# x rows of the gate and up stage in four buffers on one side, its factors emitted in turn with them, and the residual loads on GpSimd's queue

## The chip, the cores and the metric

One core of a Trainium2 chip runs the whole program. The metric is device time in microseconds (us), the median of the runs shown. Every time below is from one profiled execution of the kernel before, counted from the start of its span, if nothing else is said.

## What is computed

One layer of a hybrid decoder over 2048 prompt tokens (with 16 meta tokens ahead of them) and 32 sample tokens, all in float32. The change touches what comes after the two mixing branches are merged into `mix`:

```python
mix = (sigmoid(ga) * br_a + sigmoid(gb) * br_b) @ w_out
x = x + rms_norm(mix, norm_mix_post)
f = rms_norm(x, norm_ffn_pre)
f = (silu(f @ w_ffn_gate) * (f @ w_ffn_up)) @ w_ffn_down
x = x + rms_norm(f, norm_ffn_post)
```

D_MODEL is 1024 and D_FF is 2816. A float32 product is made of three matmuls: each operand is split into a high part (rounded to fp32r) and a low part (the rest), and high by high, high by low and low by high are summed (`mm3`, L156 to L163; in two stages written out).

## The kernel before

The stages run one after the other: projection, convolution and the two branches, merge, **way out**, **gate and up**, **down**. TensorE (PE) is busy in nearly all of them.

**Way out** (L1320 on) takes the merged rows `mg_d`, multiplies them by w_out, and goes by groups of rows: first the 32 sample rows, then eight pairs of 128 rows. For each tile `way_rows` loads `mr` (L1356, on SP's queue), splits it into `hh` (L1358, ACT) and `hl` (L1360, DVE), loads the residual rows `xr` (L1363, SP's queue) and does 48 matmuls `psr` (L1370 to L1373). `way_tail` then does a pair: a squared sum `sq` (L1394, ACT), the gain (L1399, DVE), a reciprocal root by ten or so short DVE instructions (L100 to L107), the residual sum (L1404, DVE, into `xr`), the write of y (L1405, POOL's queue), a second norm and its scaling `wa` (L1411, DVE), eight transposes of a tile on PE (L282, `pst`), their copies out `fo` (L286, ACT) and four writes of `f_d` (L287, POOL's queue). The tail of a pair runs while PE multiplies the next pair. Each engine and each queue takes its instructions in the order in which the program was built, which the program's framework makes from the emitted code and from when buffers come free.

**Gate and up** (L1505 on) computes both products with a Strassen-Winograd scheme of seven block products. Its operands are prepared by two generators. `b_parts` (L1427) loads quarters of the normed rows from `f_d` (L1434, tile `fr`, 128 x 4 x 348), splits each (`xh` L1440 on ACT, `xl` L1441 on DVE), and makes the sums that the scheme needs (L1450, L1453, L1458, L1462, DVE); the last of these needs a second load of one quarter. `a_parts` (L1467) loads a column block of both weights (L1482, `araw`) and makes the factors `ah` (L1475, ACT) and `al` (L1476, DVE or POOL), with the sums `S` and `R` (L1488 to L1491, DVE) between. The factors live in a ring of 56 KB a partition, `ar`, which is handed out from its top down; a tile `pad` taken first sets where the first factors come to lie. `gate_up` empties `b_parts` and then `a_parts` before the first step. 33 steps of some 26 us follow (three column pairs by eleven blocks of weights), each with 168 matmuls `psf`; they write `h_d` (L1547).

**Down** (L1595 on) loads rows of h (`hr`, L1621, from `h_d`, 768 KB each), splits them (`hh` L1623 on ACT, `hl` L1628 on DVE) and multiplies by split weights `wu` (`wload`: `wr` loaded at L144, high part at L146 on ACT, low part half on POOL at L148, half on DVE at L149); the matmuls are `psr`, L1637, L1638 and L1640.

The memory of a stage is taken from pools on the left and on the right side of SBUF (`run`, L1719 to L1750). A tile of a later stage may lie on memory of an earlier one, and then its first writer waits for the last reader there. In the kernel before the four buffers of `fr` are two on the right and two, `fr2`, on the left; the left two lie on `wa` tiles of the way out.

Of the kernel before, what the change touches and what calls it, by code (L numbers as in the profile page):

```python
# [7 lines left out]
F32 = mybir.dt.float32  # L8
# [7 lines left out]
P = 128  # L16
D = 1024
NM = 16
SEQ = 2048
# [24 lines left out]
PAIRS = ((0, 348), (696, 348), (1392, 344))  # L44
# [5 lines left out]
def ap_of(t, off, dims):  # L50
    return bass.AP(tensor=t.tensor, offset=t.offset + off, ap=[list(d) for d in dims])
# [19 lines left out]
class Trunk:  # L71
# [1280 lines left out]
    def way_rows(self, r, c):  # L1352
        nc, v = self.nc, self.nc.vector
        wide = r == SMP
        raw = self.wr.tile([P, 1024], F32, tag="wr", name="mr").rearrange("p (k m) -> p k m", k=8)[:, :, :r]
        nc.sync.dma_start(raw, ap_of(self.mg_d, c, [[XW, P], [P * XW, 8], [1, r]]))  # L1356
        hi = self.hh.tile([P, 8, P], F32R, tag="hh", name="hh")
        nc.scalar.activation(hi[:, :, :r], raw, AF.Copy, scale=0.25)  # L1358
        lo = hi[:, :, r:2 * r] if wide else self.hh.tile([P, 8, P], F32R, tag="hl", name="hl")
        v.scalar_tensor_tensor(lo[:, :, :r], raw, 0.25, hi[:, :, :r].bitcast(F32), op0=OP.mult, op1=OP.subtract)  # L1360
        x = self.tm.tile([P, D], F32, tag="tm", name="xr")
        src = self.io["x_prompt"] if c < SEQ else self.io["x_sample"]
        nc.sync.dma_start(x[:r], ap_of(src, c * D if c < SEQ else 0, [[D, r], [1, D]]))  # L1363
        rr = 2 * r if wide else r
        ps = self.pw.tile([P, 2, BLK], F32, tag="pw", name="psr")[:rr]
        for k, (wh, wl) in enumerate(self.wo):
            for half in range(2):
                cs = slice(BLK * half, BLK * half + BLK)
                o = ps[:, half]
                nc.tensor.matmul(o, hi[:, k, :rr], wh[:, cs], start=k == 0, stop=False)  # L1370
                nc.tensor.matmul(o, hi[:, k, :rr], wl[:, cs], start=False, stop=wide and k == 7)
                if not wide:
                    nc.tensor.matmul(o, lo[:, k, :r], wh[:, cs], start=False, stop=k == 7)  # L1373
        ps = ps.rearrange("p a b -> p (a b)")
        if wide:

            t = self.ac.tile([P, D], F32, tag="ac", name="lows")
            nc.scalar.activation(t[:rr], ps, AF.Copy)
            u = self.ac.tile([P, D], F32, tag="ac", name="lowt")
            nc.sync.dma_start(u[:r], t[r:rr])  # L1380
            nc.gpsimd.tensor_add(t[:r], t[:r], u[:r])
            ps = t
        return ps[:r], x, r, c
# [121 lines left out]
    def gate_up(self):  # L1505

        n = FF // 256
        B = None
        for B in self.b_parts(*PAIRS[0]):
            pass  # L1510
        A = [{}, {}]
        for _ in self.a_parts(0, A):
            pass
        order = [(pi, s) for pi in range(3) for s in (range(n) if pi != 1 else range(n - 1, -1, -1))]
        for (pi, s), (pj, sn) in zip(order, order[1:] + [(3, -1)]):
            An, ga = A, None
            if pj < 3 and sn != s:
                An = [{}, {}]
                ga = self.a_parts(sn, An)
            nxt = self.b_parts(*PAIRS[pj]) if pi < pj < 3 else None  # L1520
            Bn = self.gate_up_step(s, *PAIRS[pi], A, B, nxt, ga)
            A, B = An, Bn or B

    def gate_up_step(self, s, c0, w, A, B, nxt, ga):
        nc, v, gp = self.nc, self.nc.vector, self.nc.gpsimd
# [144 lines left out]
    def run(self):  # L1670
        nc, io = self.nc, self.io
        flat = lambda n: io[n].rearrange("o k n -> (o k) n")
        self.w_in, self.w_ga, self.w_gb = flat("w_in"), flat("w_s5_glu_a"), flat("w_s5_glu_b")
        self.w_go, self.w_o = flat("w_gdn_out"), flat("w_out")
        self.w_fg, self.w_fu, self.w_fd = flat("w_ffn_gate"), flat("w_ffn_up"), flat("w_ffn_down")
        G = 32
        for nm, shape in (("m_d", (17 * MS,)), ("t_d", (3 * P * 1024,)), ("on_d", (512, XW)),
                          ("zg_d", (20 * P, XW)), ("tt_d", (G, P, P)), ("wv_d", (G, P, 4, P)),
                          ("cs_d", (G, 64, 2, NL)), ("y_d", (G * 16, 8, YW)),
                          ("u_d", (G * 16, 8, UW)), ("qkv_d", (1536, QW)), ("gct_d", (17, H, P)),  # L1680
                          ("mg_d", (D, XW)), ("f_d", (D, XW)), ("h_d", (FF, XW))):
            setattr(self, nm, self.scratch(nm, shape))
        self.const = self.pool("const", 1)
        kw = dict(reuse_waits="tile")
        self.wp, self.pm, self.wo = Ring(), Ring(), []
        self.pt = self.pool("pt", 2, space=PSUM)
        with ExitStack() as lo:
            self.wr = self.pool("wr", 2, lo)
            self.wp.add(self.pool("wp", 3, lo), 3)
            with ExitStack() as pmx, ExitStack() as pgx:  # L1690
                self.pg = self.pool("pg", 16, pgx, side="right")
                self.pm.add(self.pool("pm", 3, pmx, space=PSUM), 3)
                with ExitStack() as ph:
                    self.tm = self.pool("tm", 4, ph)
                    self.cv = self.pool("cv", 11, ph)
                    self.gd = self.pool("gd", 1, ph)
                    self.small = self.pool("small", 2, ph)
                    self.p1c = self.pool("p1c", 1, ph)
                    self.gp = self.pool("gp", 3, ph, space=PSUM)
                    self.constants()  # L1700
                    self.p1()
                self.wp.add(self.pool("wp2", 5, lo, **kw), 5)
                with ExitStack() as ph:
                    self.wp.add(self.pool("wp4", 4, ph, **kw), 4)
                    self.cv = self.pool("cv2", 7, ph, side="right", **kw)
                    self.pm.add(self.pool("pm2", 3, ph, space=PSUM, **kw), 3)
                    self.merge()
            with ExitStack() as ph:
                self.hh = self.pool("hh", 2, ph, **kw)
                self.ac = self.pool("ac", 2, ph, **kw)  # L1710
                self.tm = self.pool("tm2", 4, ph, **kw)
                self.sq = self.pool("sq", 1, ph, **kw)
                self.fo = self.pool("fo", 2, ph, **kw)
                self.rows = self.pool("rows", 1, ph, **kw)
                self.small = self.pool("small2", 2, ph, **kw)
                self.pw = self.pool("pw", 3, ph, space=PSUM, **kw)
                self.way_out()
        self.pm = self.pool("pm3", 6, space=PSUM, **kw)
        with ExitStack() as ph:  # L1719
            self.gr = self.pool("gr", 2, ph, side="right", **kw)  # L1720
            self.xp = self.pool("xp", 1, ph, side="right", **kw)
            self.fr = Ring()
            self.fr.add(self.pool("fr", 2, ph, side="right", **kw), 2)
            ar = self.pool("ar", 1, ph, side="right", **kw)
            self.ar = ar.ring(56 * 1024, name="ar")
            self.ar.tile([P, 6144], F32, name="pad")
            self.gt = self.pool("gt", 1, ph, **kw)
            self.xq = self.pool("xq", 1, ph, **kw)
            self.xr = self.pool("xr", 1, ph, **kw)
            self.gs = self.pool("gs", 1, ph, **kw)  # L1730
            self.fr.add(self.pool("fr2", 2, ph, **kw), 2)
            self.gate_up()
        with ExitStack() as ph:
            self.wp = Ring()
            self.ac = self.pool("ac3", 9, ph, **kw)
            self.rows = self.pool("rows3", 1, ph, **kw)
            self.lw = self.pool("lw", 1, ph, **kw)
            self.cv = self.pool("cv3", 2, ph, **kw)
            self.small = self.pool("small3", 2, ph, **kw)
            self.wr = self.pool("wr3", 2, ph, side="right", **kw)  # L1740
            self.wp.add(self.pool("wp3", 10, ph, side="right", **kw), 10)
            self.wp.add(self.pool("wp5", 2, ph, **kw), 2)
            self.hh = self.pool("hh", 2, ph, **kw)
            self.hr = self.pool("hr", 2, ph, **kw)
            self.down()
# [202 lines left out]
```

## Time and profile before

| what | value |
|---|---|
| median of 3 runs | 3285.52 us (3281.97 to 3293.22) |
| the profiled execution, its own time | 3288.82 us |
| its span | 3287.0 us |
| PE busy | 3105.4 us, 94% of the span |
| DVE busy | 2015.5 us, 61% |
| ACT busy | 1120.6 us, 34% |
| POOL busy | 910.1 us, 28% |
| mean granted TensorE clock | 0.981 of full speed |
| gate and up stage | about 1833 to 2753 us |

A busy share is a mean over stages. PE is full in the steady part of every stage; the places where it is not are the joints between stages and a few single waits. So a change of this kind is read at the joints: which wait of PE ends last there, and what that instruction had been waiting for.

### The profile page before, as it was taken

How to read it: one execution, taken by the hardware profiler on the slowest of the kernel's cores; microseconds unless marked ns; L12 is line 12 of the kernel's file. 1: busy time of each engine (PE TensorE's matmuls, PEld its weight loads, DVE VectorE, ACT ScalarE, POOL GpSimd, SP SyncE). 2: the span in 40 equal slices, each digit the busy share in tenths (PEclk: the TensorE clock that was granted, in tenths of full speed). 3: DMA queues.
4: the chain of work that ended last, by engine and by line, in shares of the span. 5: the costliest groups of instructions: out<-in, count | busy, mean ns of one | idle time of the engine just before them, and what ended most of it. 6: DMA issues, size and time to landing. Idle time of an engine off the chain costs nothing. (4 is left out here: it accounts for less than half of the span.)

```text
span 3287.0 us, 47621 instructions
## 1 busy us (share of the span) xinstructions
PE 3105.4 (94%) x17461; PEld 2709.1 (82%) x17461; DVE 2015.5 (61%) x4648; ACT 1120.6 (34%) x1944; POOL 910.1 (28%) x903
## 2 busy tenths in 40 slices
PE   6998999999999999999999699999999999999998
PEld 5887778877777777988777699999999998887776
DVE  6888854657897546553444766676676664246235
ACT  4633222433232224221233444444444444223211
POOL 1123441123332212201111344434434444122110
PEclk9999999999999999999999799999999999999999
DMA  5336456545465435653553433333333334235224
GB/s 118 123 101 178 123 156 182 123 122 149 140 190 168 126 110 156 189 158 119 176 180 127 154 104 104 103 121 104 103 103 107 103 103 134 92 102 141 82 59 69
DMA packets 469018, 419.30 MB, mean 128 GB/s; under 512 B 120794, under 2 KB 393370, under 8 KB 468784
## 3 DMA queue, kind: packets, MB, share of 16 engines
q1 hardware_dynamic: 458576, 382.18, 39.9%
q0 software_dynamic: 10208, 34.09, 3.7%
q8 instruction: 137, 2.24, 0.3%
q14 instruction: 97, 0.79, 0.1%
HBM read 288.27 MB, written 127.65 MB: 127 GB/s over the span
## 5 line engine op out<-in xcount | busy, mean ns | idle before, releaser
L161 PE MATMUL psf<-xh,ah 128*128 128x348 f32 (+1 forms) x1848 | 598.8, 324 | 31.9 <-ACT sn L1534 20.2
L163 PE MATMUL psf<-xh,al 128*128 128x348 f32 (+1 forms) x1848 | 593.2, 321 | 6.8 <-DVE al L1476 6.8
L162 PE MATMUL psf<-xl,ah 128*128 128x348 f32 (+1 forms) x1848 | 593.0, 321 | 0.0
L161 PEld LDWEIGHTS psf<-xh,ah 128*128 128x128 f32 x1848 | 348.1, 188 | 41.5 <-ACT sn L1534 29.0
L163 PEld LDWEIGHTS psf<-xh,al 128*128 128x128 f32 x1848 | 347.6, 188 | 7.1 <-DVE al L1476 7.1
L162 PEld LDWEIGHTS psf<-xl,ah 128*128 128x128 f32 x1848 | 348.1, 188 | 0.0
L161 PE MATMUL psg<-pgh,wh 128*128 128x512 f32 (+1 forms) x800 | 300.0, 375 | 1.3 <-ACT wh L146 1.3
L1638 PE MATMUL psr<-wu,hh 128*128 128x512 f32 (+2 forms) x748 | 295.4, 395 | 4.2 <-POOL wu L148 4.2
L163 PE MATMUL psg<-pgh,wl 128*128 128x512 f32 (+1 forms) x800 | 291.4, 365 | 6.0 <-DVE wl L149 5.2
L1637 PE MATMUL psr<-wu,hh 128*128 128x512 f32 (+2 forms) x748 | 294.3, 395 | 0.0
L162 PE MATMUL psg<-pgl,wh 128*128 128x512 f32 (+1 forms) x800 | 291.3, 364 | 0.0
L1640 PE MATMUL psr<-wu,hl 128*128 128x512 f32 x704 | 277.6, 395 | 0.0
L148 POOL TENSOR_TENSOR wl<-wr,wh 128x512 fp32r<-128x512 f32 x92 | 143.8, 1563 | 389.5 <-ACT wh L146 318.9
L161 PE MATMUL psq<-pgh,wh 128*128 128x512 f32 (+1 forms) x480 | 180.4, 376 | 0.3 <-ACT pgh L268 0.3
L163 PEld LDWEIGHTS psg<-pgh,wl 128*128 128x128 f32 x800 | 155.5, 195 | 30.3 <-DVE wl L149 5.4
L1476 POOL TENSOR_TENSOR al<-R,ah 128x1024 fp32r<-128x1024 f32 x62 | 162.8, 2626 | 50.4 <-ACT ah L1475 50.4
L161 PEld LDWEIGHTS psg<-pgh,wh 128*128 128x128 f32 x800 | 156.0, 195 | 23.7 <-issue 2.9
L162 PEld LDWEIGHTS psg<-pgl,wh 128*128 128x128 f32 x800 | 155.9, 195 | 22.0 <-issue 2.5
L1638 PEld LDWEIGHTS psr<-wu,hh 128*128 128x128 f32 (+2 forms) x748 | 137.7, 184 | 42.9 <-POOL wu L148 6.7
L163 PE MATMUL psq<-pgh,wl 128*128 128x512 f32 (+1 forms) x480 | 172.9, 360 | 0.0
L162 PE MATMUL psq<-pgl,wh 128*128 128x512 f32 (+1 forms) x480 | 172.6, 360 | 0.0
L1637 PEld LDWEIGHTS psr<-wu,hh 128*128 128x128 f32 (+2 forms) x748 | 137.6, 184 | 35.9
(497 smaller groups left out, 6733.9 us busy)
## 6 DMA issues: line engine op xcount, KB each, us to landing
wr<-w_in SPq DMA_DIRECT2D x72, 512.0 KB
araw<-w_ffn_gate SPq DMA_DIRECT2D x31, 1024.0 KB
araw<-w_ffn_up SPq DMA_DIRECT2D x31, 1024.0 KB
wr<-w_ffn_down SPq DMA_DIRECT2D x44, 512.0 KB
zg_d<-gt SPq DMA_DIRECT2D x80, 256.0 KB
h_d<-hm SPq DMA_DIRECT2D x44, 348.0 KB
qkv_d<-cy SPq DMA_DIRECT2D x48, 256.0 KB
hr<-h_d SPq DMA_DIRECT2D x16, 768.0 KB
```

Of the source, the lines that this page charges most:

```text
L148: nc.gpsimd.tensor_sub(lo[:, :c], raw[:, :c], hi[:, :c].bitcast(F32))
L161: t.matmul(ps, wh, xh, start=first, stop=False, **kw)
L162: t.matmul(ps, wh, xl, start=False, stop=False, **kw)
L163: t.matmul(ps, wl, xh, start=False, stop=last, **kw)
L1476: eng.tensor_sub(flat(lo), x, flat(hi).bitcast(F32))
L1637: nc.tensor.matmul(ps, hi[:, k, cl], wh[:, cs], start=k == 0, stop=False)
L1638: nc.tensor.matmul(ps, hi[:, k, cl], wl[:, cs], start=False, stop=both and k == n - 1)
L1640: nc.tensor.matmul(ps, lo[:, k, c - c0:c - c0 + r], wh[:, cs], start=False, stop=k == n - 1)
```

## The change

It does four things.

1. The 17 loads of `xr` (L1363) go from SP's queue to POOL's.
2. `fr` has four buffers in one pool on the right; the two on the left are gone.
3. The ring `ar` begins lower, because `fr` now takes more of the right side, and `pad` is 7936 floats a partition in place of 6144.
4. `gate_up` takes the first two parts of `b_parts`, then the first two of `a_parts` (the factors a11 and a12 of gate and up), and then the rest of both in turn.

```diff
@@ way_rows
-        nc.sync.dma_start(x[:r], ap_of(src, c * D if c < SEQ else 0, [[D, r], [1, D]]))
+        nc.gpsimd.dma_start(x[:r], ap_of(src, c * D if c < SEQ else 0, [[D, r], [1, D]]))
@@ gate_up
-        B = None
-        for B in self.b_parts(*PAIRS[0]):
-            pass
-        A = [{}, {}]
-        for _ in self.a_parts(0, A):
+        A, B = [{}, {}], None
+        xs, ws = self.b_parts(*PAIRS[0]), self.a_parts(0, A)
+        next(xs), next(xs)
+        next(ws), next(ws)
+        for B in xs:
+            next(ws, None)
+        for _ in ws:
             pass
@@ run
-            self.fr = Ring()
-            self.fr.add(self.pool("fr", 2, ph, side="right", **kw), 2)
+            self.fr = self.pool("fr", 4, ph, side="right", **kw)
             ar = self.pool("ar", 1, ph, side="right", **kw)
             self.ar = ar.ring(56 * 1024, name="ar")
-            self.ar.tile([P, 6144], F32, name="pad")
+            self.ar.tile([P, 7936], F32, name="pad")
...
-            self.fr.add(self.pool("fr2", 2, ph, **kw), 2)
```

From `gate_up` on, the lines of the changed kernel have numbers larger by two (L1547 is L1549, L1621 is L1623, L1623 is L1625).

The built programs differ at four places. At the start of the way out, the first loads of `araw` go on SP's queue ahead of the first loads of `mr` and of `lowt` (the low half of the sample rows); before, they stood behind them. In the tail of the second pair, DVE now does three sums of x rows. The names are those of the kernel: `wrs` is the reciprocal root, `fr` and `t` x rows, `hl` the low part of the next tile of the way out. DVE there, before:

```order
L105 SCALAR_TENSOR_TENSOR rst<-rsy 128x2
L106 TENSOR_TENSOR rst<-rst,rsx 128x2
L107 SCALAR_TENSOR_TENSOR wrs<-rst,rsy 128x2
L1411 TENSOR_SCALAR wa<-xr,wrs 128x1024 x2
L1360 SCALAR_TENSOR_TENSOR hl<-mr,hh 128x1024 x2
```

And DVE now:

```order
L106 TENSOR_TENSOR rst<-rst,rsx 128x2
L1453 TENSOR_TENSOR t_17742<-fr 128x1392
L107 SCALAR_TENSOR_TENSOR rsy<-rst,rsy 128x2
L1360 SCALAR_TENSOR_TENSOR hl<-mr,hh 128x1024
L105 SCALAR_TENSOR_TENSOR rst<-rsy 128x2
L1458 TENSOR_TENSOR fr<-fr 128x1392
L106 TENSOR_TENSOR rst<-rst,rsx 128x2
L107 SCALAR_TENSOR_TENSOR wrs<-rst,rsy 128x2
L1411 TENSOR_SCALAR wa<-xr,wrs 128x1024 x2
L1360 SCALAR_TENSOR_TENSOR hl<-mr,hh 128x1024
```

L1450 stands some ten rows further up, behind L1404. L1450 waits for the third load of `fr`, L1453 for the fourth; L1411, on which PE's transposes of this pair wait, is behind both. On PE 22 matmuls of the next tile stand ahead of these transposes (4 before).

At the end of the way out, on ACT, before:

```order
L1394 ACTIVATE sq,wss<-psr 128x1024
L286 ACTIVATE fo<-pst,c_norm_ffn_pre 128x256 x6
L1394 ACTIVATE sq,wss<-xr 128x1024 x2
L286 ACTIVATE fo<-pst,c_norm_ffn_pre 128x256 x8
L1440 ACTIVATE xh<-fr 128x1392 x2
L1440 ACTIVATE xh<-t_17733 128x1392
L1475 ACTIVATE ah<-araw 128x1024 x2
```

And ACT now:

```order
L286 ACTIVATE fo<-pst,c_norm_ffn_pre 128x256 x4
L1440 ACTIVATE xh<-t_17742 128x1392
L1440 ACTIVATE xh<-fr 128x1392
L286 ACTIVATE fo<-pst,c_norm_ffn_pre 128x256 x2
L1440 ACTIVATE xh<-fr 128x1392 x2
L1440 ACTIVATE xh<-t_17742 128x1392
L1394 ACTIVATE sq,wss<-xr 128x1024 x2
L286 ACTIVATE fo<-pst,c_norm_ffn_pre 128x256 x8
L1475 ACTIVATE ah<-araw 128x1024 x2
```

Five splits of x rows moved ahead of the last pair's `sq`; the first factors `ah` are where they were, behind the last `fo`. DVE does likewise: between L1399 and L1404 of the last pair it now has four `xl` and, after them, L1462, which waits for the second load of a quarter; that load waits for the second of these `xl`.

At the start of down, on SP's queue, before (two loads of `hr` had been issued long ahead, in the middle of gate and up):

```order
L144 DMA wr<-w_ffn_down 128x1024
L1621 DMA hr<-h_d 128x6x256 x2
L1547 DMA h_d<-hm 128x688
L1750 DMA row<-norm_ffn_post 128x1024
L1547 DMA h_d<-hm 128x688
L144 DMA wr<-w_ffn_down 128x1024 x8
```

And SP now:

```order
L144 DMA wr<-w_ffn_down 128x1024
L1549 DMA h_d<-hm 128x688
L1750 DMA row<-norm_ffn_post 128x1024
L1549 DMA h_d<-hm 128x688
L144 DMA wr<-w_ffn_down 128x1024 x2
L1623 DMA hr<-h_d 128x6x256
L144 DMA wr<-w_ffn_down 128x1024 x2
L1623 DMA hr<-h_d 128x6x256 x2
```

All loads of `hr` now stand at the end, the first behind the third and fourth `wr`. PE's first matmul of down needs `hh` of that first `hr`.

## Rows read from the trace of the kernel before

**Rows 1.** Busy time by stretch: stretch, length, PE, PEld, DVE, ACT, POOL, clock, DMA share, GB/s.

```profile
1590.00:1620.00 30.00, 27.95 (x122) 20.63 (x120) 14.25 (x37) 7.27 (x10) 3.45 (x3) 1.00 0.72 225
1799.00:1826.00 27.00, 10.55 (x50) 8.11 (x48) 11.84 (x33) 8.96 (x20) 5.53 (x9) 0.70 0.34 113
1826.00:1850.00 24.00, 9.29 (x37) 8.55 (x38) 22.55 (x14) 12.13 (x13) 8.33 (x4) 0.63 0.64 206
2780.00:2800.00 20.00, 20.00 (x88) 16.05 (x87) 5.38 (x6) 8.16 (x10) 7.20 (x4) 1.00 0.66 214
```

**Rows 2.** Timeline, ACT, way out: start, us, line, names, [idle before <-releaser].

```profile
1674.59 1.06 ACT L1358 ACTIVATE hh<-mr 128x1024 fp32r<-128x1024 f32 x1 [8.47 <-PE psr L1371]
...
1705.46 1.06 ACT L1358 ACTIVATE hh<-mr 128x1024 fp32r<-128x1024 f32 x1 [4.83 <-PE psr L1371]
...
1730.04 1.06 ACT L1358 ACTIVATE hh<-mr 128x1024 fp32r<-128x1024 f32 x1 [8.49 <-PE psr L1371]
```

**Rows 3.** Timeline, all engines, tail of the first pair.

```profile
1681.65 2.48 DVE L1404 SCALAR_TENSOR_TENSOR xr<-wa,wrs,xr 128x1024 f32<-128x1024 f32 x2
...
1687.03 0.36 SPq L1434 DMA_DIRECT2D fr<-f_d  x1
...
1692.21 1.36 ACT L1440 ACTIVATE xh<-fr 128x1392 fp32r<-128x1392 f32 x1 [4.37 <-DMA fr<-f_d]
...
1695.20 1.22 DVE L1360 SCALAR_TENSOR_TENSOR hl<-mr,hh 128x1024 fp32r<-128x1024 f32 x1
...
1696.92 1.42 DVE L1411 TENSOR_SCALAR wa<-xr,wrs 128x1024 f32<-128x1024 f32 x2
...
1697.82 0.45 PE L282 MATMUL pst<-ident,wa 128*128 128x128 f32 x1 [5.74 <-DVE wa L1411]
```

**Rows 4.** The same view, tail of the second pair.

```profile
1712.52 2.48 DVE L1404 SCALAR_TENSOR_TENSOR xr<-wa,wrs,xr 128x1024 f32<-128x1024 f32 x2
...
1718.65 1.42 DVE L1411 TENSOR_SCALAR wa<-xr,wrs 128x1024 f32<-128x1024 f32 x2
...
1719.55 0.30 PE L282 MATMUL pst<-ident,wa 128*128 128x128 f32 x1 [0.70 <-DVE wa L1411]
```

**Rows 5.** The same view, end of the way out and start of gate and up.

```profile
1810.81 2.48 DVE L1404 SCALAR_TENSOR_TENSOR xr<-wa,wrs,xr 128x1024 f32<-128x1024 f32 x2
...
1825.92 0.72 POOL L287 DMA_DIRECT2D f_d<-fo  x1 [0.39 <-ACT fo L286]
...
1832.36 1.99 ACT L1475 ACTIVATE ah<-araw 128x1024 fp32r<-128x1024 f32 x2
...
1835.15 3.12 DVE L1441 TENSOR_TENSOR xl<-fr,xh 128x1392 fp32r<-128x1392 f32 x2
...
1838.18 3.75 DVE L1462 TENSOR_TENSOR t<-fr,t 128x1392 f32<-128x1392 f32 x1
...
1844.19 0.66 PE L163 MATMUL psf<-xh,al 128*128 128x348 f32 x1 [6.79 <-DVE al L1476]
```

**Rows 6.** Timeline, start of down; SP's first loads of hr are far ahead.

```profile
2459.91 0.96 SPq L1621 DMA_DIRECT2D hr<-h_d  x2
...
2743.76 2.87 ACT L1623 ACTIVATE hh<-hr 128x1536 fp32r<-128x1536 f32 x2 [0.29 <-PE psf L163]
...
2755.06 2.95 POOL L148 TENSOR_TENSOR wu<-wr,wu 128x512 fp32r<-128x512 f32 x2
...
2756.82 0.50 PE L1638 MATMUL psr<-wu,hh 128*128 128x512 f32 x1 [2.95 <-POOL wu L148]
...
2762.88 1.06 ACT L146 ACTIVATE wu<-wr 128x1024 fp32r<-128x1024 f32 x1 [1.44 <-DMA wr<-w_ffn_down]
```

**Rows 7.** Timeline, SP's and POOL's queues in the tail of the third pair.

```profile
1744.06 1.02 SPq L1363 DMA_DIRECT2D xr<-x_prompt  x2
...
1746.43 0.72 POOL L287 DMA_DIRECT2D f_d<-fo  x1 [6.00 <-ACT fo L286]
```

**Rows 8.** DMA issues in the way out: names, queue, count, KB each, median us to landing.

```profile
f_d<-fo POOLq DMA_DIRECT2D x32, 256.0 KB, 4.0
```

## The prediction

> **What bounds the kernel now.** I read the busy time by stretch first, since it finds the places where TensorE isn't full: in a steady stretch it is (20.00 of 20 us in down, clock 1.00), in the joint between the way out and gate and up it is not: 10.55 of 27 us and then 9.29 of 24, at clocks of 0.70 and 0.63 [rows 1]. Then the timelines of these places, for the wait that ends last. Three matter here.
>
> First, the way out. A pair takes 24.58 us from one `hh` to the next (1705.46 to 1730.04), but the one from 1674.59 took 30.87 [rows 2]. What lies in between is the first pair's tail [rows 3]: DVE is behind a load of x rows issued at 1687.03 whose split on ACT began at 1692.21, so L1411 came at 1696.92, 15.27 after its L1404; a pair later the distance is 6.13 [rows 4]. L1411 was 9.14 late, and PE idled 5.74 in place of 0.70 [rows 3, 4]. So 4.1 of the lateness was covered by matmuls of the next tile, and the pair lost 30.87 - 24.58 = 6.3 us in all, some 1.2 of it behind the wait.
>
> Second, the joint [rows 5]: the last `f_d` write is issued at 1825.92, the first factors `ah` come at 1832.36 behind x rows, and PE runs without gaps only from 1844.19, after `al`.
>
> Third, the start of down [rows 6]: two loads of h had been issued at 2459.91, `hh` was ready at 2743.76 + 2.87 = 2746.6, and PE idled only 2.95 us before 2756.82, for the first weights.
>
> **The change, term by term.**
>
> *A second stall in the way out.* Two more loads of x rows now land during it, and DVE's sums on them stand in the second pair's tail ahead of L1411. That pair has the first pair's timing 30.87 us later (L1404 at 1681.65 and 1712.52 [rows 3, 4]), and SP issues the fourth load on the same condition, the pair's last `f_d` write. So I take the first pair's distances: issue 1712.52 + 5.38 = 1717.9, data 5.18 later at 1723.1 [rows 3]. Then L1453 (1.56, as an `xl` of the same tile, 3.12 for two [rows 5]), `hl` 1.22 [rows 3], L1458 1.56, and four short steps, some 0.7 (between the end of `hl` and L1411 three took 0.5 [rows 3]): L1411 at 1728.1 instead of 1718.65, 9.5 late. With the same 22 matmuls ahead of the transposes, cover is again 4.1, which leaves 5.4 and the 1.2 behind it. Bounds: 0 (the load lands in the pair's slack) and +6.6; I take the measured 6.3 of the first pair.
>
> *The joint.* Off the path after the last `f_d`: the third and fourth loads, three sums, five splits. But four `xl` (3.12 for two) and L1462 (1.6 like an `xl`, or 3.75 as it took [rows 5]) move between L1399 and L1404 of the last pair, and L1462 waits for a load that is issued only after the second of these `xl`. Two `xl` 3.1, then 5.2 for the load, which covers the other two and most of the root, less about 2 us of root that DVE did there anyway, then L1462 1.6: L1404 is late by 3.1 + 5.2 - 2 + 1.6 = 7.9. All behind it shifts: last `f_d` issue 1825.92 + 7.9 = 1833.8, landing 4.0 later [rows 8], 1837.8. The first factors don't gain by the new memory: by the tile addresses of the built program they lie on `fo`, `xr` and `wa` tiles of the way out (a ring that is handed out downwards, with a larger `pad`, ends lower, not on free memory), and the first `ah` waits for the last `f_d` write. So `ah` 1.0 (1.99 for two [rows 5]) ends at 1838.8, and no x row is missing. PE begins there at the lower clock, as at this joint before (0.63 [rows 1]); behind the first pair's 5.7 us of idling that cost 1.2, after a longer idle I take 1.7. That is worth a full-speed start at 1840.5, against 1844.2 before (the few matmuls done ahead of 1844.19 about pay for the lower clock behind it). Gain -3.7. If the tail were not late at all, -3.7 - 7.9 = -11.6; if L1462 takes 3.75 and its load queues for another 2.6, +1.
>
> *The start of down.* The new place of the ring covers the buffers of `hr`, so its loads stand behind the third and fourth `wr`. The first `wr` of these goes when POOL has done `wu` twice, from 2755.06 for 2.95: 2758.0 for the second [rows 6]. `hr` then issues at 2758.4, beside a `wr` of 512 KB whose split began at 2762.88 before; an x load of 696 KB took 5.18 alone [rows 3], `hr` has 768 KB, and both together I put at 6 to 8: 2764.4 to 2766.4. `hh` 1.4 (2.87 for two [rows 6]): PE at 2765.8 to 2767.8 instead of 2756.82, 9 to 11 late; behind it the lower clock again (+1.7), minus short waits for weights that vanish, at most as much (`wu` followed PE closely there [rows 6]). I take +10; +6 if the data come by 2762.5, +13 if `hr` queues fully behind two `wr`. PE is full afterwards [rows 1], so none of it comes back.
>
> *The first weight loads* now precede `lowt` and the first `mr` at the start of the way out. 2 MB more at the front of a stretch that moves 225 GB/s, where PE works 27.95 of 30 us [rows 1]: 0 if they are through before `lowt` is due, at most one of them, 1.05 MB at 225 GB/s = 4.7. The row is nearer to nothing: +1.
>
> *The x loads on POOL.* They wait, as on SP, for the y write and L1411 of their buffer: 1744.06 for both [rows 7]. At 0.72 each, like POOL's `f_d` issue, they are off by 1745.5, 0.9 before POOL's next `f_d` at 1746.43 [rows 7]; on SP they leave a queue that isn't late. [...] The nearest row on landing is that POOL's writes land in 4.0 us [rows 8], with DVE at work in the same tails. [...]
>
> *Gate and up's steady steps* keep their order: 0.
>
> Sum: 6.3 - 3.7 + 10 + 1 = +13.6, so 3302.4 for an execution like the profiled one (3288.82; its span 3287.0 and 1.8 around it). That one lies 3.3 above the median of the runs, so I predict 3285.5 + 13.6 = 3299. A measurement of this kernel tells some 0.3%, 9.9 us, from no change (its runs lie 11 apart).
>
> **Rivals.**
>
> *The second stall is covered.* If the fourth load is in by 1713 (its `f_d` writes are out earlier than I think), DVE's three sums cost 1.56 each, 4.7 late, and 4.1 of cover leaves 0.6. Then 13.6 - 5.7 = +7.9, 3293: within 0.3%. For it: the loads wait on nothing else. Against: the first pair, where the same form of wait cost 6.3.
>
> *The tail isn't pushed* (the other side). Place: DVE between L1399 and L1404 of the last pair. If the four `xl` and L1462 ran where DVE waits anyway, the joint gives its full -11.6; the same early data leave no second stall; with down at its lower end, +6, and nothing at the start, the sum is -5.6 and the time 3280, not slower. Should the pairs also lose the 0.70 that PE idles in each [rows 4], 8 x 0.70 = 5.6 more, it is 3274. It decides at the last `f_d` issue: by 1826 it holds, by 1834 it doesn't. Against: the order puts the load behind an `xl` that itself waits for L1399.
>
> [...]
>
> *The change doesn't do what it says.* Its first factors don't lie in free memory; if the x rows are also as late as before and `hr` turns out early, all that is left is about +1: 3287.
>
> **How the numbers follow.** The forecast 0.55, of which 0.48 over 0.3% and 0.07 within; second stall covered 0.18, within; tail not pushed 0.15, of which 0.06 faster by over 0.3% and 0.09 within; POOL late 0.07, slower; nothing happens 0.05, within. So faster 0.06, same 0.39, slower 0.55. The range goes from 3283, which leaves out most of the tail rival and the lower bounds together, to 3308, the upper end of down and of the start; it leaves out about 2 in 10.
>
> **What would show it.** In the changed profile: the first L1638 of down waiting some 10 us more than the 2.95, on ACT's `hh`; a wait of 5 us on L1411 ahead of the second pair's transposes, as in the first; the last `f_d` issue 8 us later against the last way-out matmul; `ah` right after it and no second gap at `al`. PE's first matmul of down within 4 us of the last `psf`, or the last `f_d` where it was, would make the prediction wrong.

## The result, and the profile after

The changed kernel takes 3307.24 us (median of 7 runs, 3301.52 to 3313.42), beside 3293.22 us for the kernel before (7 runs, 3281.97 to 3299.83): ratio of the runs 1.0053 (the medians alone give 1.0043), 95% interval 1.0036 to 1.0069, so slower by 12 to 23 us. Forecast were 3299 us and +13.6 us.

The profiled executions (span 3287.0 before, 3305.0 after) are compared by segments. Marks are ACT's `hh` L1358 in the way out (the sample rows' is number 0, the pairs' are 1 to 16) and DVE's last `su` of gate and up. What the prediction calls the first, second and third pair of the way out are, counted by these marks, the third, fourth and fifth of its eight pairs.

| segment (us) | before | after | difference | predicted |
|---|---|---|---|---|
| start of span to `hh` 0 | 1589.18 | 1585.25 | -3.9 | 0 |
| start of the way out, `hh` 0 to 8 | 85.41 | 92.54 | **+7.1** | +1 |
| first stall, `hh` 8 to 10 | 30.87 | 31.97 | +1.1 | 0 |
| second stall, `hh` 10 to 12 | 24.58 | 31.21 | +6.6 | +6.3 |
| last pairs, `hh` 12 to 16 | 49.13 | 49.13 | 0 | 0 |
| joint with gate and up, `hh` 16 to last `su` | 974.04 | 970.63 | -3.4 | -3.7 |
| down, last `su` to the end | 533.79 | 544.27 | +10.5 | +10 |

From `hh` 0 to the end the change costs 21.9 us. The first line varies from execution to execution by up to 17 us, whatever the kernel (last section), so it is kept apart. One segment is far from its term: the start of the way out.

Lines of the changed kernel's page (span; PE's busy time; the costliest group of down: busy, mean ns of one, idle time before it and what ended it):

```profile
span 3305.0 us, 47593 instructions
...
PE 3112.8 (94%) x17461; PEld 2715.9 (82%) x17461; DVE 2019.9 (61%) x4648; ACT 1120.3 (34%) x1944; POOL 915.9 (28%) x920
...
L1639 PE MATMUL psr<-wu,hh 128*128 128x512 f32 (+2 forms) x748 | 296.4, 396 | 13.7 <-ACT hh L1625 13.7
```

PE is busy 7.4 us longer than before; the rest of the 18 us between the spans is idling. The 13.7 us are one wait, at the start of down.

**Start of the way out.** Timeline of the kernel before (start, us, engine, line, names, [idle before <-releaser]):

```profile
1604.04 0.62 SPq L1380 DMA_DIRECT2D lowt<-lows  x1
...
1606.68 0.57 SPq L1482 DMA_DIRECT2D araw<-w_ffn_gate  x1
1607.30 1.66 SPq L1482 DMA_DIRECT2D araw<-w_ffn_up  x1
...
1606.68 2.38 POOL L1381 TENSOR_TENSOR lows<-lows,lowt 32x1024 f32<-32x1024 f32 x1 [9.91 <-DMA lowt<-lows]
...
1620.43 0.31 PE L282 MATMUL pst<-ident,wa 32*128 32x32 f32 x2 [1.36 <-DVE wa L1411]
```

And of the changed one:

```profile
1575.50 0.38 SPq L1482 DMA_DIRECT2D araw<-w_ffn_gate  x1
...
1594.49 0.80 SPq L1482 DMA_DIRECT2D araw<-w_ffn_up  x1
1600.11 0.76 SPq L1380 DMA_DIRECT2D lowt<-lows  x1
...
1608.67 2.38 POOL L1381 TENSOR_TENSOR lows<-lows,lowt 32x1024 f32<-32x1024 f32 x1 [14.78 <-DMA lowt<-lows]
...
1621.36 0.42 PE L282 MATMUL pst<-ident,wa 32*128 32x32 f32 x2 [5.54 <-DVE wa L1411]
```

`lowt` is 128 KB. Before, its consumer ran 2.64 us after the issue; now, with 1 MB of `araw` (the load of 1594.49) and the x rows ahead of it, 8.56 us after. The other load of `araw` went out 24.6 us ahead of `lowt`, and the first two of `mr`, at 1570.65, ahead of both. The whole chain of the sample rows (`lows`, root, L1404, L1411) hangs on it, and PE waits 5.54 us for L1411 in place of 1.36: of the 5.9 us, 4.2 became waiting. Busy time by stretch of the changed kernel, as in [rows 1], shows what came behind that wait:

```profile
1590.00:1620.00 30.00, 24.71 (x108) 18.11 (x106) 12.07 (x32) 7.39 (x10) 4.50 (x5) 1.00 0.65 190
...
1599.25:1602.25 3.00, 3.00 (x15) 2.48 (x14) 1.18 (x1) 1.78 (x2) 0.00 (x0) 1.00 1.04 312
1602.25:1605.25 3.00, 3.00 (x15) 2.46 (x15) 0.04 (x1) 0.00 (x0) 0.00 (x0) 1.00 1.08 333
...
1620.25:1623.25 3.00, 1.89 (x6) 1.54 (x7) 0.98 (x3) 0.46 (x2) 1.23 (x2) 0.62 0.08 19
1623.25:1626.25 3.00, 3.00 (x9) 2.32 (x8) 0.00 (x0) 0.00 (x0) 0.06 (x1) 0.50 0.50 172
1626.25:1629.25 3.00, 3.00 (x12) 2.37 (x11) 0.00 (x0) 0.00 (x0) 0.00 (x0) 0.75 0.00 0
1629.25:1632.25 3.00, 3.00 (x16) 2.01 (x15) 1.23 (x1) 2.61 (x7) 0.91 (x2) 1.00 0.02 5
```

For the first 5 us that `lowt` is under way the DMA engines are full (1.04, 1.08; in the next 3 us it is 0.78). After PE's 5.54 us of idling the granted clock falls to 0.50 and is back at 1.00 some 6 us later. Busy time times (1 - clock) gives 0.72 + 1.50 + 0.75 = 3.0 us; with 5.54 - 1.36 = 4.2 more of waiting that is 7.2, the segment's 7.1. Before, after 1.36 us of idling, the clock stayed at 1.00:

```profile
1621.18:1624.18 3.00, 3.00 (x14) 2.45 (x14) 0.00 (x0) 0.06 (x1) 0.75 (x1) 1.00 0.62 186
```

**Second stall.** Timeline of the changed kernel, fourth pair's tail; its counterpart is [rows 4]:

```profile
1716.81 2.48 DVE L1404 SCALAR_TENSOR_TENSOR xr<-wa,wrs,xr 128x1024 f32<-128x1024 f32 x2
1720.38 1.61 DVE L1450 TENSOR_TENSOR fr<-fr 128x1392 f32<-128x1392 f32 x1 [1.08 <-DMA fr<-f_d]
...
1726.84 1.61 DVE L1453 TENSOR_TENSOR t<-fr 128x1392 f32<-128x1392 f32 x1 [3.39 <-DMA fr<-f_d]
...
1729.64 1.60 DVE L1458 TENSOR_TENSOR fr<-fr 128x1392 f32<-128x1392 f32 x1
...
1731.54 1.42 DVE L1411 TENSOR_SCALAR wa<-xr,wrs 128x1024 f32<-128x1024 f32 x2
...
1732.44 0.45 PE L282 MATMUL pst<-ident,wa 128*128 128x128 f32 x1 [5.20 <-DVE wa L1411]
...
1732.87 1.20 POOL L1363 DMA_DIRECT2D xr<-x_prompt  x2 [12.72 <-DVE wa L1411]
```

L1411 comes 14.73 us after L1404 instead of 6.13, so it is 8.6 late (9.5 were predicted), and PE idles 5.20 instead of 0.70. That is 4.5 of the segment's 6.6; the other 2.1 come behind the wait, where the clock is at 0.50 until 1735 and at 0.67 until 1738.

**Joint.** The same view, end of the way out; its counterpart is [rows 5]:

```profile
1827.49 1.61 DVE L1462 TENSOR_TENSOR t<-fr,t 128x1392 f32<-128x1392 f32 x1 [0.24 <-DMA fr<-f_d]
1829.02 2.47 DVE L1404 SCALAR_TENSOR_TENSOR xr<-wa,wrs,xr 128x1024 f32<-128x1024 f32 x2
...
1843.27 1.44 POOL L287 DMA_DIRECT2D f_d<-fo  x2 [2.97 <-ACT fo L286]
...
1846.83 2.00 ACT L1475 ACTIVATE ah<-araw 128x1024 fp32r<-128x1024 f32 x2 [3.13 <-DMA f_d<-fo]
...
1847.94 0.66 PE L161 MATMUL psf<-xh,ah 128*128 128x348 f32 x1 [7.37 <-ACT ah L1475]
1860.43 0.43 PE L161 MATMUL psf<-xh,ah 128*128 128x348 f32 x1 [0.31 <-ACT sn L1536]
```

`hh` 16 is at 1779.17 before and at 1790.10 after. Measured from there L1404 is at 38.92 instead of 31.64, 7.3 late (7.9 were predicted). `ah` follows the last `f_d` and waits for it, and there is no second gap at `al`. PE begins 57.84 us after `hh` 16 (59.6 were worked out), and the lower clock behind it (0.50 until 1850 and 0.75 until 1856) costs 2.5 (1.7).

The segment holds all 33 steps. In a step ACT copies products of PE (`sn`) and DVE adds others to them (`su`, six to a step); the `su` tell where the difference arises. By the last `su` of the first step the changed kernel is 4.1 us ahead, by that of the second 2.6, by that of the last 3.4. In the second step PE waits 1.83 us for an `sn`, and the clock falls behind it; in e10, the run with the old `pad`, the same wait of 1.92 us leaves it at 1.00. Stretches of the changed kernel, then of e10:

```profile
1884.00:1890.00 6.00, 4.17 (x26) 3.88 (x25) 3.72 (x7) 1.63 (x4) 2.60 (x1) 1.00 0.79 271
1890.00:1896.00 6.00, 6.00 (x30) 6.00 (x29) 1.61 (x3) 2.06 (x4) 1.85 (x1) 0.72 0.00 0
...
1890.00:1896.00 6.00, 4.08 (x26) 3.79 (x25) 4.65 (x7) 2.14 (x4) 2.17 (x2) 1.00 0.57 199
1896.00:1902.00 6.00, 6.00 (x40) 6.00 (x39) 3.10 (x5) 2.44 (x4) 1.01 (x1) 1.00 0.00 0
```

The fall costs 6.00 x 0.28 = 1.7 us. It is in all four executions with the new `pad` and all else of gate and up as changed (changed, e3, e4, e9: their joints take 969.83 to 971.63 us, e10's 967.59); why there and not in e10 is not shown.

**Start of down.** Timeline and two stretches of the changed kernel, to be held against [rows 6] (before, the clock stayed at 1.00 there):

```profile
2763.94 2.00 SPq L144 DMA_DIRECT2D wr<-w_ffn_down  x2
2765.99 0.43 SPq L1623 DMA_DIRECT2D hr<-h_d  x1
...
2772.90 1.48 ACT L1625 ACTIVATE hh<-hr 128x1536 fp32r<-128x1536 f32 x1 [1.10 <-DMA hr<-h_d]
...
2774.43 0.80 PE L1639 MATMUL psr<-wu,hh 128*128 128x512 f32 x1 [13.74 <-ACT hh L1625]
```

```profile
2769.00:2775.00 6.00, 0.56 (x1) 0.50 (x2) 1.51 (x3) 2.72 (x3) 3.12 (x2) 0.50 0.83 258
2775.00:2781.00 6.00, 6.00 (x21) 4.53 (x20) 3.55 (x3) 3.42 (x3) 3.16 (x2) 0.74 1.01 350
```

The last `su` is at 2753.21 before and 2760.73 after. From it to the first `hr` issue are 5.3 us, from that to `hh` 6.9, and PE starts 13.7 after the `su`. Before, its first three matmuls of down stood right behind the last `psf`, and the wait for weights behind them ended 3.6 after the `su`. The clock at 0.74 costs 1.6 behind the new wait.

### The profile page after: what moved, and what is told of

It reads as the page before. It is cut to its first block, busy times and chain, and to the rows that moved or that the text cites. A ratio compares the mean times of both kernels' runs of the same rounds, so it can differ in the third digit from the quotient of the medians.

```text
span 3305.0 us, 47593 instructions
## 1 busy us (share of the span) xinstructions
PE 3112.8 (94%) x17461; PEld 2715.9 (82%) x17461; DVE 2019.9 (61%) x4648; ACT 1120.3 (34%) x1944; POOL 915.9 (28%) x920
## 4 chain that ended last, share of the span: by engine, by line
PE 65%; DVE 13%; issue 11%; DMA 5%; ACT 3%; POOL 2%; SPq 1%; POOLq 0%; ACTq 0%; DVEq 0%
PE psf L161 8%; PE psf L163 8%; PE psf L162 8%; PE psg L162 3%; PE psg L163 3%; PE psg L161 3%; PE psr L1639 2%; PE psr L1640 2%; PE psr L1642 2%; DVE cy L395 1%; PE psq L161 1%; PE psq L162 1%; PE psq L163 1%; PE psgo L163 1%; PE psga L163 1%
## 5 line engine op out<-in xcount | busy, mean ns | idle before, releaser
L1639 PE MATMUL psr<-wu,hh 128*128 128x512 f32 (+2 forms) x748 | 296.4, 396 | 13.7 <-ACT hh L1625 13.7
```

The lines of the kernel that those rows point to most:

```text
L1639: nc.tensor.matmul(ps, hi[:, k, cl], wh[:, cs], start=k == 0, stop=False)
```

## The experiments

All segments are from profiled executions, in the order of the table above; ratios are to the kernel before.

| run | start | 1st stall | 2nd stall | joint, g+u | down | ratio, 95% interval |
|---|---|---|---|---|---|---|
| before | 85.41 | 30.87 | 24.58 | 974.04 | 533.79 | |
| changed | 92.54 | 31.97 | 31.21 | 970.63 | 544.27 | 1.0053 (1.0036 to 1.0069) |
| e1 | 92.30 | 31.90 | 24.56 | 973.82 | 534.7 | 1.0013 (0.9996 to 1.0030) |
| e2 | 85.31 | 32.64 | 31.47 | 968.02 | 545.26 | 1.0029 (1.0012 to 1.0046) |
| e3 | 92.06 | 32.03 | 31.38 | 971.63 | 529.95 | 1.0013 (0.9996 to 1.0029) |
| e4 | 89.81 | 31.55 | 31.10 | 969.83 | 544.2 | 1.0042 (1.0024 to 1.0061) |
| e5 | 85.38 | 30.85 | 32.55 | 969.51 | 529.69 | 0.9985 (0.9969 to 1.0001) |
| e6 | 85.39 | 32.74 | 24.56 | 969.88 | 529.70 | 0.9972 (0.9954 to 0.9989) |
| e7 | 85.32 | 24.57 | 24.57 | 969.25 | 529.70 | 0.9936 (0.9909 to 0.9963) |
| e8 | 85.33 | 24.57 | 24.57 | 967.49 | 529.59 | 0.9931 (0.9911 to 0.9951) |
| e9 | 85.36 | 32.19 | 31.37 | 970.58 | 543.64 | 1.0042 (1.0023 to 1.0062) |
| e10 | 89.77 | 31.82 | 31.20 | 967.59 | 545.87 | one run |
| e11 | 85.32 | 24.56 | 24.57 | 966.73 | 529.51 | 0.9940 (0.9918 to 0.9961) |

### One part alone

**e1**: the kernel before with only the x rows' loads on POOL.

```diff
-        nc.sync.dma_start(x[:r], ap_of(src, ...))
+        nc.gpsimd.dma_start(x[:r], ap_of(src, ...))
```

> The kernel before with one part of the change: the 17 loads of xr on POOL's queue. Theory (four terms: start of the way out +7, second stall +6.6, joint -3.4, start of down +10): the loads of the residual rows only matter because SP's queue, rid of them, issues the first two weight loads ahead of lowt. So lowt lands some 6 us late, the first transposes wait about 5.5 us instead of 1.4, and the pairs keep 24.6 us; no second stall, no late hr: +7 us over the kernel before. Rival (the queue itself costs): the pairs get longer by 0.5 us or more each, f_d writes come later behind the loads, +4 or more beyond the start. Rival 2 (nothing but the buffers matters): within 2 us of before.

The start has the whole loss (+6.9: `lowt` took 8.24 us, PE waited 5.25), the fourth pair and all after it keep 24.56. So this one line causes the loss at the start, without the other three edits; and POOL as a queue costs nothing in the pairs. The segments show it (+8.6 us from `hh` 0 to the end); in time e1 can't be told from the kernel before.

**e9**: the other way round, the changed kernel with this one line undone.

> The changed kernel with the x rows' loads back on SP (that one line undone), all else as changed. Theory (the whole loss at the start of the way out comes from this line: without it the gate factors' loads stand behind lowt again): start of the way out 85.4 instead of 92.5, first pst's wait 1.3 instead of 5.5 and no drop of the granted clock behind it, second stall, joint and down as in the changed kernel (31.2, -3.4, +10.5 against the kernel before), time 6 to 8 us below the changed kernel. Rival (the places or the order of gate and up's first loads are what delays lowt): start stays at 90 to 92.5 and the time within 2 us of the changed kernel.

The start is back at 85.36; PE's wait in the timeline of this run, and the stretch behind it, at clock 1.00:

```profile
1630.68 0.31 PE L282 MATMUL pst<-ident,wa 32*128 32x32 f32 x2 [1.26 <-DVE wa L1411]
```

```profile
1631.53:1634.53 3.00, 3.00 (x15) 2.45 (x14) 0.00 (x0) 0.00 (x0) 0.75 (x1) 1.00 0.61 186
```

All other segments are the changed kernel's. From `hh` 0 to the end it is 7.5 us shorter (1712.27 against 1719.75), as expected. The times do not show it: 3310.92, no lower than 3307.24. The ratios, 1.0042 and 1.0053, have intervals wide enough for the full 7 us as well as for nothing. The segments decide here, and on the time the expectation was not met.

**e4**: the changed kernel with both loads of `araw` queued behind `lowt`.

```diff
-            nc.sync.dma_start(u[:r], t[r:rr])
+            self.lowt = nc.sync.dma_start(u[:r], t[r:rr])
...
+            with self.tc.issue_after(self.lowt.ins):
                 nc.sync.dma_start(raw, ap_of(w, 256 * s, ...))
```

> The changed kernel with the first two weight loads (araw) queued on SP behind lowt; xr loads stay on POOL. Theory: lowt lands about 2.6 us after its issue instead of 8.6, the first transposes wait about 1.4 us instead of 5.5, and 5 to 7 us of the start come back; all else as in the changed kernel. Rival (lowt is late because of the xr loads that POOL now issues at the same place, or because of POOL's own add): lowt still lands over 6 us after its issue and nothing comes back.

`lowt` took 4.36 us instead of 8.56, so 4.2 of the 5.9 more are `araw`'s. But the start gave back only 2.7 of 7.1: PE still idled 3.07 us, and behind it the clock was 0.50, 0.50 and 0.86 in three slices of 3 us, in which busy time times (1 - clock) is again 2.9. Less idling saved the idling, and nothing of the clock, so the expected 5 to 7 us were missed:

```profile
1617.17:1620.17 3.00, 2.04 (x6) 1.69 (x7) 0.87 (x2) 0.47 (x2) 1.29 (x2) 0.50 0.58 152
1620.17:1623.17 3.00, 3.00 (x8) 2.32 (x8) 0.00 (x0) 0.00 (x0) 0.00 (x0) 0.50 0.44 167
1623.17:1626.17 3.00, 3.00 (x13) 2.42 (x13) 0.00 (x0) 0.00 (x0) 0.00 (x0) 0.86 0.00 0
```

That is not a rule: in e10 a wait of 4.16 us here cost only 1.7 at the lower clock (0.55 and 0.88 in two slices of 3 us). The remaining 1.7 of `lowt`'s delay is put down to the x rows on POOL, which now start before it; that was not tried by itself.

**e2**: the kernel before with only the four places of `fr` on the right; x rows on SP, pad and order as before.

```diff
-            self.fr = Ring()
-            self.fr.add(self.pool("fr", 2, ph, side="right", **kw), 2)
+            self.fr = self.pool("fr", 4, ph, side="right", **kw)
...
-            self.fr.add(self.pool("fr2", 2, ph, **kw), 2)
```

> The kernel before with the other part: four fr buffers on the right, xr loads on SP, old emission and old pad. Theory: start as before (first transposes wait about 1.4 us), second pair 31.2 us long with a wait of about 5.9 us on L1411, gap-free start of gate and up 3.4 us earlier against the last way-out matmul, first matmul of down waiting for hh, 10 us later against the last psf: +13 us over the kernel before. Rival (emission and pad do part of it): the joint or the start of down differ from the changed kernel by more than 1 us.

Second stall, joint and the late `hr` all come from this edit. Its joint, 968.02, is 2.6 better than the changed kernel's, which is the rival's sign: the pad or the order of emission costs something there. e10 tells them apart.

**e10**: the changed kernel with the old `pad`; the same instructions in the same order, at other addresses.

```diff
-            self.ar.tile([P, 7936], F32, name="pad")
+            self.ar.tile([P, 6144], F32, name="pad")
```

> The changed kernel with the pad of 6144 of the kernel before: the same instructions in the same order on every engine, only addresses differ. Theory (the changed pad lays the first weight factors on fo, xr and wa of the way out, so that ACT's first ah waits for the last f_d; that costs the 2.6 us by which the joint is worse than with four right fr places alone): hh16 to the last su 968 instead of 970.6, no [<-DMA f_d] wait on the first ah. Rival (the order in which gate and up's first parts are written makes the difference): it stays at 970 to 971. Down stays at 544.

The joint is 967.59, 3.0 shorter than the changed kernel's, and the first `ah` follows the last `fo` at once, though the second of them now has a short wait for an `f_d` write (ACT's timeline):

```profile
1849.19 1.05 ACT L1475 ACTIVATE ah<-araw 128x1024 fp32r<-128x1024 f32 x1
1851.43 1.06 ACT L1475 ACTIVATE ah<-araw 128x1024 fp32r<-128x1024 f32 x1 [1.18 <-DMA f_d<-fo]
```

So the new pad costs the joint some 3 us, in this one execution; the order of emission is not the cause (e2, with the old order and the old pad, has 968.02). By the `su`, 1.4 of it are there by the end of the first step, and 1.5 come in the second, where the clock falls only with the new pad. The start, +4.4 here with the same order of loads as in the changed kernel (`lowt` 7.16 us, PE's wait 4.16), shows how much that loss varies between executions.

### Mending one wait after the other

**e3**: the changed kernel with `hr` laid on the memory of `fr`, between two parts of down's weight pool, so that its first loads need not wait for the ring.

```diff
-            self.wp.add(self.pool("wp3", 10, ph, side="right", **kw), 10)
+            self.wp.add(self.pool("wp3", 4, ph, side="right", **kw), 4)
+            self.hr = self.pool("hr", 2, ph, side="right", **kw)
+            self.wp.add(self.pool("wp4", 6, ph, side="right", **kw), 6)
...
-            self.hr = self.pool("hr", 2, ph, **kw)
```

> The changed kernel with the two hr buffers of down on the right, between two parts of the wu pool, where they lie on the fr buffers of gate and up, which are free long before the end. Theory: two hr loads go out in the middle of gate and up again, hh is ready ahead of the last steps, PE's wait at the start of down is about 3 us instead of 13.7, and the time is 10 us under the changed kernel (+7 to +8 over before). Rival (the start of down is held by the weights anyway, hr only stands in front of them): the wait passes to wu, and less than 4 us come back.

Two loads of `hr` are far ahead again, as in [rows 6], `hh` is ready before gate and up ends, and down takes 14.3 us less than in the changed kernel. That is 3.8 less than in the kernel before, and not for `hr` alone: the edit moves weight buffers too, SP issues six `wr` ahead of the last `su` instead of two, and PE's longest wait for weights is 0.83 us instead of 2.95:

```profile
2474.07 1.87 SPq L1623 DMA_DIRECT2D hr<-h_d  x2
...
2762.10 2.85 ACT L1625 ACTIVATE hh<-hr 128x1536 fp32r<-128x1536 f32 x2
```

**e5**: the kernel before with the edits of e2 and e3 together.

> The kernel before, with two edits alone: all four fr places on the right (as in the change) and the hr places laid on their memory, between two parts of the down pool; xr stays on SP, order and pad of gate and up as before. Theory (the costs of the parts add, and the place of hr is the whole of the loss in down): against the kernel before, start of the way out 0, first stall +1 to +2, second stall +6.6, hh16 to the last su -6.0, down -3.8, together -1 to -3 us. Rival (with the way out as it is, hr's memory next to fr costs something elsewhere, or down's gain was part of the other edits): down +5 to +11, together +5 us or more.

The parts add, roughly: from `hh` 0 to the end -0.7 us against the kernel before (-1 to -3 expected), down -4.1. The second stall is +8.0 here, and the joint -4.5 instead of the expected -6.0: with `hr` in its new place the last step of gate and up takes 1.0 to 1.3 us longer (e3, e5 to e8).

**e6**: e5, with the three sums of `b_parts` issued behind the last L1411 of a later tail. `scaled` lists the L1411s from the sample rows' on, so that index 10 is the fifth pair's; the expectations of this run and the next count one lower.

```diff
+        with self.behind(c0, self.scaled, 10):
             v.tensor_sub(b11, b12, b11)
...
+        with self.behind(c0, self.scaled, 10):
             v.tensor_sub(t2, b22, b11)
...
+        with self.behind(c0, self.scaled, 10):
             v.tensor_sub(b12, b22, b12)
```

> The run with fr and hr edited, and the sums L1450, L1453 and L1458 of the first b_parts, with what follows them, issued behind the fourth pair's last L1411. Theory (the second stall is DVE's waits for fr in L1450 and L1453, standing ahead of the fourth pair's L1404 and L1411): the second stall goes (24.6 us instead of 31.2), and as the chain to gate and up stands later in DVE's order at most 1 us of it comes back at the tail: -7 to -9 us against the kernel before. Rival (the stall is only moved: the fifth pair's L1404 then waits for the same fr loads): the next hh interval is 6 us longer, time -1 to -3 us.

The second stall is gone and none comes behind it: -6.4 us from `hh` 0 to the end (-7 to -9 expected; the first stall is 1.9 longer than in e5).

**e7**: e6, with the splits of the first two quarters (parts of b11 and b21) in the same way behind the fourth pair's last L1411 and a square before it.

> The run before it, and the parts (L1475 to L1478 of the way out's side) of the first two quarters issued behind the third pair's last square and L1411 instead of ahead of them. Theory (the stall that the kernel before has too, 5.74 us on PE at 1697.82, is the splits' wait for the first fr loads on ACT and DVE): it goes (24.6 us instead of 30.9): -13 to -16 us against the kernel before. Rival (x of the third pair or the DMA is late there, not the splits): that interval stays at 30 to 32, time as in the run with the sums alone.

The first stall, which the kernel before has too, goes as well (PE's timeline of this run, third and fourth pair):

```profile
1681.97 0.30 PE L283 MATMUL pst<-ident,wa 128*128 128x128 f32 x1 [0.68 <-DVE wa L1412]
...
1706.54 0.30 PE L283 MATMUL pst<-ident,wa 128*128 128x128 f32 x1 [0.68 <-DVE wa L1412]
```

From `hh` 0 to the end that is -15.3 us against the kernel before, and 0.64% in time.

**e8**: e7, with the last sum (L1462) and the splits of the four sums and of b22 behind the way out's last L1411.

> The run before it, and the last sums and splits of the first b_parts (t2, t1, t3, t4, b22) issued behind the last L1411 of the way out. Theory (the tail's L1404 is held by the four xl splits and L1462 on DVE; freed, its L1411 and ah are some 7.5 us earlier, and PE needs only ah and the first quarter): hh16 to the last su 5 to 8 us shorter than in the run before it, -18 to -23 us against the kernel before, 0.6 to 0.7% faster. Rival (gate and up then waits for these splits itself in its first products): the gap only moves behind the first psf; time within 2 us of the run before it.

The rival was right: 1.8 us in the joint, not 5 to 8. L1411 came 7.8 us earlier (PE waits 11.28 for it, 19.11 in e7), but PE's second gap, for `al`, ended 58.1 us after `hh` 16 in both.

**e11**: e8 without a pad, so that the first factors lie above the way out's tiles, with the change's order of emission, and t4 and b22 behind the first two `al`.

> The run with the tail freed, without any pad (the first factors then lie above the way out's own tiles), with the first parts of gate and up written interleaved as in the change, and t4 and b22 behind the first two al. Theory (what is left at the joint is ACT's and DVE's own order: ah behind the last fo, al behind the splits and behind f_d): the wait of 4.24 us for al goes, ah comes 1 to 2 us earlier, hh16 to the last su 4 to 6 us shorter (962 to 964 instead of 967.5): 1 to 1.2% below no run yet, 0.8 to 0.9% faster than the kernel before. Rival (the first products then wait for t4 and b22 or the second factors instead): within 2 us of the run with the tail freed.

(The clause "below no run yet" in it has no meaning.) The wait of 4.24 us for `al` is gone (one of 1.23 comes later) and PE is full at clock 1.00 some 10 us earlier than in e8, yet the joint is only 0.8 shorter. Stretches of e11, columns as above:

```profile
1834.76:1840.76 6.00, 6.00 (x40) 6.00 (x38) 6.00 (x3) 1.80 (x2) 5.90 (x3) 1.00 0.11 12
1840.76:1846.76 6.00, 3.50 (x20) 2.92 (x20) 6.00 (x7) 3.76 (x5) 1.66 (x1) 1.00 1.02 338
...
1868.76:1876.76 8.00, 5.32 (x30) 5.03 (x29) 5.69 (x9) 3.35 (x6) 4.17 (x3) 0.89 0.70 221
1876.76:1884.76 8.00, 8.00 (x47) 8.00 (x46) 3.76 (x5) 2.47 (x4) 1.63 (x1) 0.90 0.00 0
```

The start is given back in the first two steps: PE catches up with DVE, which is full (6.00 of 6), and idles 2.5 of 6 us, then 2.7 more at the next step with the clock down to 0.89. What PE waits for behind 1840.76 stands behind sums and `al` on DVE; for the later gap, DVE itself had idled 2.28 us for an `al` of POOL. So the joint is bound there by the making of the factors, on DVE and then POOL, and not by PE's start. e7, e8 and e11 cannot be told apart in time; all three beat both kernels by more than the 0.3% that can be told.

## Why the prediction was right or wrong

**Direction and range.** Slower by over 0.3% was the likeliest case, and it is what happened; 3307.24 lies just inside the range. +13.6 us is inside the measured 12 to 23, and the median of the kernel before rose by 7.7 us with more runs (3285.52 to 3293.22), which is most of the 8 us between 3299 and 3307. That agreement is partly luck: from `hh` 0 on the profile shows +21.9, and the sum of the terms misses 8.3 of it, 6.1 in the first weight loads, 1.1 in the first stall and the rest in small parts.

**The step that failed** is the term of the first weight loads, "+1", with "at most one of them, 1.05 MB at 225 GB/s = 4.7" as its bound. It measured +7.1 (e1 +6.9; e10, with the same order, +4.4). Two things were wrong in it. The row was held to be nearer to nothing, because PE worked 27.95 of 30 us there [rows 1]; but of the missing 2.05 us, 1.12 were a wait for the first `hl` and the rest the first 0.93 of the 1.36 us wait at the end of the sample rows' chain. PE was waiting for that chain already, so little covered a later `lowt`. And the bound priced the wait alone. It held for that (4.2 more), but the clock behind it cost 3.0 again; the prediction had counted this very effect at the three other places (1.2 to 1.7 each) and left it out here. The cause, as e1 and e9 show, is the move of the x rows off SP's queue: the `araw` loads, which stood behind them, moved ahead of `lowt`. The prediction named that move of loads, but its sum has no term for "The x loads on POOL" apart from it.

In e4, with `araw` behind it and the x rows on POOL's queue started before it, `lowt` still took 4.36 us, against 2.64 in the kernel before; whether the x rows make that difference was not tried by itself.

**Second stall**: +6.6 against +6.3; e2 has it with the places of `fr` alone, e6 takes it away by moving the three sums. Right in mechanism and sum; its two parts, 5.4 and 1.2, came out as 4.5 and 2.1.

**First stall**: +1.1, not in the prediction. It is between 30.85 and 32.74 in every run that has it, and e5, with the edits of e2 that should lengthen it, has the 30.85; its cause was not tested.

**Joint**: -3.4 against -3.7. The late L1404 (7.3 of 7.9), the first `ah` waiting for the last `f_d`, no second gap: the path is as worked out, and by the end of the first step it gave -4.1. That the whole segment ends 0.3 from the term is luck in part: the fall of the clock in the second step took 1.5 back, and the later steps gave 0.8. e10 shows that the new addresses, which the prediction read, cost 3.0 us, 1.4 by the wait for `f_d` at the start and 1.5 in the second step. The rival "the tail isn't pushed" put 7.9 on the pushed tail; e8, which frees it, got 1.8. That price was wrong: `al` and the splits behind it on DVE are late next.

**Start of down**: +10.5 against +10, from the places of `fr` (e2) by way of `hr`'s memory (e3). Right.

**POOL's queue**: the sum has no term for it, and the pairs show none: 24.56 us for the fourth pair in e1, and 49.13 from `hh` 12 to 16 before and after. The x loads wait for L1411 themselves, and POOL issues two in 1.20 us as it ends; where the second goes 2.77 us behind the first (1780.06 and 1782.83), that segment is no longer for it. No run shows a pair that a late queue makes longer, for which the forecast had 0.07.

**Steady steps**: 0 was predicted. From the third step on the changed kernel gains 0.8 us over 31 steps; e2, with the places of `fr` alone, gains as much, e1 only 0.1. Its cause was not tested. The 1.5 us lost in the second step are the clock's, as said.

## What to carry to other kernels

When loads leave a queue, list what moves up in it: a small load on which a chain hangs can end up behind megabytes (here the consumer of `lowt`, 128 KB, ran 8.56 us after its issue in place of 2.64). A gap of PE has a second price where the granted clock falls behind it (here up to 3.0 us, behind a wait of 5.54), so a term for a wait needs both, with a bound for the second. A new memory place is free only if the first writer there has nothing to wait for (here the first `ah` waited 3.13 us for an `f_d` write), and each tile that it pushes elsewhere must be followed to its own next reader (here `hr`, for whose `hh` PE waited 13.74 us).

## What had not been expected

The part of the program ahead of `hh` 0, where no run altered more than the place of one weight load, ended between 1582.6 and 1599.9 us in the 13 profiled executions. In the eight that were followed in ACT's timeline, the largest part arises between 416 and 590 us (where a spread of 5 us grows to 13) and stays from there. So single executions differ by up to 0.5% for nothing, the kernel before has 3285.52 as the median of 3 runs and 3293.22 of 7, and a change behind that part is better read from a mark at its start.

What the clock costs behind a gap of PE does not follow the gap's length here: 2.9 us behind 3.07 us of idling (e4), 1.7 behind 4.16 (e10), 3.0 behind 5.54 (changed), 1.7 behind 1.83 (changed, second step), and nothing behind 1.36 (before) and 1.92 (e10, second step). What decides it is not shown.
